# Strassen MLP of a two-layer backbone: in the last chunk pair the second token group goes first, and the block sums of the second matrix no longer trail the chunk pairs

## The chip, the cores and the metric

One core of one Trainium2 chip runs the whole program in one launch. The metric is device time in microseconds (us). The core has a matrix engine (TensorE; PE in the rows, with its weight loads as PEld), two elementwise engines (VectorE, DVE; ScalarE, ACT), GpSimd (POOL), and SyncE (SP), which issues all DMA transfers here, one after the other in its own queue.

## The reference, cut to what matters

Two layers over 1,024 latent and 256 context tokens of width 1,024. Each layer has a token mixer (a gated short convolution in layer 0, a bidirectional mLSTM in layer 1) and then a dense MLP with a squared ReLU; before and after each there is an RMSNorm with shift, scale and gate. Only the MLP matters here:

```
def _sqrelu_mlp(h, w1, w2):
    return jnp.square(jax.nn.relu(h @ w1)) @ w2
```

w1 is 1,024 x 4,096 and w2 is 4,096 x 1,024. Layer 0 runs it on 1,280 tokens, layer 1 on the 1,024 latent ones. Everything is float32.

## The kernel before

Both matrix products of the MLP are done with a Strassen-Winograd scheme: each operand is cut into 2 x 2 blocks, seven products of sums of blocks take the place of eight, and each product is made of three passes over a high part and a rest (so a float32 number goes to TensorE as two pieces).

**The first product** is `mlp_up` (lines 488 to 509). The 4,096 hidden columns are worked off in 16 chunk pairs, q = 0 to 15 (`NQ` = 16); "chunk pair" is a pair of 128-column chunks of w1. The tokens lie in SBUF as two groups of prepared sums, A0 and A1: 384 and 256 columns in layer 0, 256 and 256 in layer 1. In each chunk pair `up_weights` loads two blocks of w1 (`raw`, line 406) and makes seven weight pieces of them (`w`, lines 122 and 123, eight slots); then `up_group` (line 426) runs the seven products for A0 and the seven for A1, each 12 matmuls (line 433), into the PSUM tiles psX, psY, psZ, psW, psX, psZ, psW in that order. ScalarE and VectorE add up, apply the squared ReLU and form seven result pieces in one tile `st` (lines 448 to 468); the transfer on line 469 writes them to `hid_d` in DRAM. A0's group has its `st` in the pool S1, A1's in the pool M, each pool with one buffer: the first write of the next `st` of a pool (line 448, ScalarE) waits until the transfer of line 469 has read the one before.

**Block sums of w2.** `down_sums` (lines 471 to 486) makes the sums that the second product needs: for k = 0 to 15 it loads two rows of w2 (`rw`, line 476, one buffer each), does four VectorE subtractions (lines 480 to 483) and writes the results to `t_d` (lines 484 to 486). The next loads of `rw` wait until these writes have read the buffers. In the loop, chunk pair q does the sums of k = q - 2; those of 14 and 15 come after the loop.

**The second product** is `mlp_down` (from line 511). It takes the seven products one after the other (i = 1, 6, 5, 7, 4, 2, 3); for each it goes through k = 0 to 15: `w_piece` loads a block of w2 or `t_d` (line 521), `h_piece` loads a piece of `hid_d` (`hr`, line 529, three buffers) and makes high part and rest (`hp`, lines 530 and 531, four buffers), and line 536 multiplies them for five pairs of token tiles (layer 0; 15 matmuls for each k) or four (layer 1; 12) into the PSUM tiles `psd`. Lines 544 to 558 empty `psd` at the end of each of the seven.

**What sets the order.** The program is written in the order above, but a scheduler sets the order on each engine; within an engine, and in SP's queue, instructions then run strictly in that order. Memory is given out by a stack of pools: `mlp_up` holds S1 and A1 on the left and A0 and M on the right, and `mlp_down` lays its pools Y and H where S1 and A1 were. H holds `hr` and `hp`, and lies within the place of A1. So the first `hr` loads must wait until the last matmul that reads A1.

Of the kernel before, what the change touches and what calls it, by code (L numbers as in the profile page):

```python
# [37 lines left out]
def hybrid_kernel(  # L38
# [53 lines left out]
    acc = ctx.enter_context(pool("acc", bufs=6, space=PSUM))  # L92
# [306 lines left out]
    NQ = DFF // P // 2  # L399

    def up_weights(l, q, M=None):

        raw = []
        for j in range(2):
            r = rawp.tile([P, 1024], F32, tag="raw", name="raw")
            nc.sync.dma_start(r, w1[l, 2 * q + j])
            raw.append(r)
        (b11, b21), (b12, b22) = [(r[:, 0:512], r[:, 512:1024]) for r in raw]
        if M is None:
            tw = rawp.tile([P, 1024], F32, tag="raw", name="tw0")  # L410
            t2, t3 = tw[:, 0:512], tw[:, 512:1024]
        else:
            t2, t3 = [M.tile([P, 512], F32, tag="tw", name="tw", bufs=2) for _ in range(2)]
        w = {1: piece(b11)}
        nc.vector.tensor_sub(t3, b22, b12)
        nc.vector.tensor_sub(b12, b12, b11)
        nc.vector.tensor_sub(t2, b22, b12)
        w[6] = piece(t2)
        w[5] = piece(b12)
        w[7] = piece(t3)  # L420
        w[2] = piece(b21)
        w[3] = piece(b22)
        nc.vector.tensor_sub(b21, b21, t2)
        w[4] = piece(b21)
        return w

    def up_group(l, q, w, A, n, c0, pl, acc):


        def prod(ps, i, first):  # L430
            for k in range(4):
                for j, (a, b) in enumerate(PASSES):
                    nc.tensor.matmul(  # L433
                        ps,
                        w[i][:, a, k * P : (k + 1) * P],
                        A[:, PIECE[i], b, k, :],
                        start=(first and k == 0 and j == 0),
                        stop=(k == 3 and j == 2),
                        skip_group_check=not first,
                    )  # L440

        bank = lambda nm: acc.tile([P, 512], F32, tag="acc", name=nm)[:, 0:n]
        st = pl.tile([P, 7, n], F32, tag="st7", name="st7", bufs=1)
        r11, r12, r22, c21, u2 = [st[:, i] for i in (0, 1, 2, 5, 6)]
        X, Y, Z, W = bank("psX"), bank("psY"), bank("psZ"), bank("psW")
        add = nc.vector.tensor_add
        prod(X, 1, True)
        nc.scalar.copy(u2, X)  # L448
        prod(Y, 6, True)
        add(u2, Y, u2)  # L450
        prod(Z, 5, True)
        add(r22, Z, u2)  # L452
        prod(W, 7, True)
        add(r22, W, r22)  # L454
        prod(X, 2, False)
        prod(Z, 3, False)
        prod(W, 4, False)
        nc.scalar.activation(r11, X, AF.Relu)
        add(r12, Z, u2)
        add(c21, W, u2)  # L460
        nc.scalar.activation(r11, r11, AF.Square)
        for c in (r22, r12, c21):
            nc.scalar.activation(c, c, AF.Relu)  # L463
            nc.scalar.activation(c, c, AF.Square)
        add(st[:, 3], c21, r22)
        nc.vector.tensor_sub(st[:, 4], st[:, 3], r11)
        nc.vector.tensor_sub(st[:, 5], r11, c21)
        nc.vector.tensor_sub(st[:, 6], r12, st[:, 4])
        nc.sync.dma_start(hid_d[l, :, q, :, c0 : c0 + n].rearrange("s p n -> p s n"), st)

    def down_sums(l, k, M):

        r = []
        for j in range(2):
            r.append(M.tile([P, 1024], F32, tag=f"rw{j}", name="rw", bufs=1))
            nc.sync.dma_start(r[j], w2[l, (2 * k + j) * P : (2 * k + j + 1) * P, :])
        (b11, b12), (b21, b22) = [(x[:, 0:512], x[:, 512:1024]) for x in r]
        t3 = M.tile([P, 512], F32, tag="tw", name="t3", bufs=2)
        sub = nc.vector.tensor_sub
        sub(t3, b22, b12)  # L480
        sub(b12, b12, b11)
        sub(b22, b22, b12)
        sub(b21, b21, b22)
        nc.sync.dma_start(t_d[l, k, :, 3], t3)
        nc.sync.dma_start(t_d[l, k, :, 2], b12)
        nc.sync.dma_start(t_d[l, k, :, 0:2], r[1].rearrange("p (a b) -> p a b", a=2))

    def mlp_up(l, As, sX, left, S1, acc):


        (A0, n0), (A1, n1) = As
        w = up_weights(l, 0)
        up_group(l, 0, w, A0, n0, 0, S1, acc)
        w = up_weights(l, 1)
        for f in left:
            f(A1)
        up_group(l, 1, w, A0, n0, 0, S1, acc)
        sX.close()
        with pool("M", bufs=1, side="right") as M:
            up_group(l, 1, w, A1, n1, n0, M, acc)  # L500
            w = up_weights(l, 0, M)
            up_group(l, 0, w, A1, n1, n0, M, acc)
            for q in range(2, NQ):
                w = up_weights(l, q, M)
                down_sums(l, q - 2, M)
                up_group(l, q, w, A0, n0, 0, S1, acc)
                up_group(l, q, w, A1, n1, n0, M, acc)
            down_sums(l, NQ - 2, M)
            down_sums(l, NQ - 1, M)

    def mlp_down(l, pairs, xsrc, finish, T, H, Y, acc, G):

# [105 lines left out]
    with ExitStack() as s0:  # L618
# [147 lines left out]
        A0 = sA.enter_context(pool("A0", bufs=1, side="right")).tile([P, 7, 2, 4, 384], F32R, name="A0")  # L766
# [12 lines left out]
        with pool("S1", bufs=1) as S1, pool("A1", bufs=1) as pA1:  # L779
            A1 = pA1.tile([P, 7, 2, 4, 256], F32R, name="A1")  # L780
            mlp_up(0, ((A0, 384), (A1, 256)), sX, left, S1, acc)
# [337 lines left out]
    A0 = sA.enter_context(pool("A2", bufs=1, side="right")).tile([P, 7, 2, 4, 256], F32R, name="A2")  # L1119
# [12 lines left out]
    with pool("S3", bufs=1) as S1, pool("A3", bufs=1) as pA1:  # L1132
        A1 = pA1.tile([P, 7, 2, 4, 256], F32R, name="A3")
        mlp_up(1, ((A0, 256), (A1, 256)), sX, left, S1, acc)
# [78 lines left out]
```

## Time and profile before

| | |
|---|---|
| median of 3 runs | 2582.22 us (2580.07 to 2582.91) |
| profiled execution | 2577.89 us |
| its span, first to last instruction | 2576.1 us |
| mean granted TensorE clock | 0.989 of full speed |
| PE busy | 2488.1 us, 97% of the span |
| PEld busy | 2199.3 us, 85% |
| DVE busy | 1651.6 us, 64% |
| ACT busy | 1143.7 us, 44% |
| 16 DMA engines, mean | 177 GB/s |

All times in the views are in us from the start of the span of the one profiled execution. A timeline row gives start, length, engine, line, operation, the tiles written and read, and how many instructions were merged; in square brackets stands how long the engine was idle before it and what ended that. A window row gives, for each engine, busy time and number of instructions, then the granted TensorE clock (1.00 is 2.4 GHz, 0.50 is 1.2 GHz), the busy share of the DMA engines and GB/s. Matmuls overlap: 12 of 128 x 256 start within 1.43 us, though the row that merges them is 1.59 us long.

### The profile page before, as it was taken

How to read it: one execution, taken by the hardware profiler on the slowest of the kernel's cores; microseconds unless marked ns; L12 is line 12 of the kernel's file. 1: busy time of each engine (PE TensorE's matmuls, PEld its weight loads, DVE VectorE, ACT ScalarE, POOL GpSimd, SP SyncE). 2: the span in 40 equal slices, each digit the busy share in tenths (PEclk: the TensorE clock that was granted, in tenths of full speed). 3: DMA queues.
4: the chain of work that ended last, by engine and by line, in shares of the span. 5: the costliest groups of instructions: out<-in, count | busy, mean ns of one | idle time of the engine just before them, and what ended most of it. 6: DMA issues, size and time to landing. Idle time of an engine off the chain costs nothing.

```text
span 2576.1 us, 38825 instructions
## 1 busy us (share of the span) xinstructions
PE 2488.1 (97%) x14520; PEld 2199.3 (85%) x14520; DVE 1651.6 (64%) x3058; ACT 1143.7 (44%) x2503; POOL 107.0 (4%) x229
## 2 busy tenths in 40 slices
PE   8999999999999999999999899999999999999998
PEld 5888887899999988888879788887789999978886
DVE  5777784687676664445864745546578787654565
ACT  5311112565445443334654444345456555444443
POOL 1000000100000000000111100000010000000010
PEclk9999999999999999999999899999999999999999
DMA  8456663436565676555751322222336777876675
GB/s 295 132 175 189 200 194 116 136 127 231 208 242 208 225 268 199 173 167 170 234 185 51 73 78 58 66 74 83 117 126 213 252 246 259 268 239 188 184 230 182
DMA packets 230207, 454.87 MB, mean 177 GB/s; under 512 B 17802, under 2 KB 109242, under 8 KB 230018
## 3 DMA queue, kind: packets, MB, share of 16 engines
q1 hardware_dynamic: 230018, 452.38, 54.2%
q8 instruction: 114, 1.87, 0.3%
q14 instruction: 75, 0.61, 0.1%
HBM read 326.78 MB, written 125.33 MB: 176 GB/s over the span
## 4 chain that ended last, share of the span: by engine, by line
PE 53%; issue 30%; DVE 6%; DMA 6%; ACT 3%; POOL 2%; DVEq 0%; POOLq 0%; SPq 0%; ACTq 0%
PE psd L536 12%; PE op L371 5%; PE psZ L433 4%; PE psW L433 4%; PE psX L433 4%; PE psv L865 3%; PE psc L129 3%; PE pso L129 3%; DMA Dm<-nm_d 3%; PE psb L129 3%; PE psu L129 3%; PE psY L433 2%; DMA mraw<-in_mod_w_dram 2%; PE psq L129 1%; DVE macc L220 1%
## 5 line engine op out<-in xcount | busy, mean ns | idle before, releaser
L536 PE MATMUL psd<-w,hp 128*128 128x512 f32 x3024 | 712.1, 397 | 10.8 <-ACT hp L530 10.8
L536 PEld LDWEIGHTS psd<-w,hp 128*128 128x128 f32 x3024 | 573.5, 190 | 145.7 <-ACT hp L530 11.9
L531 DVE TENSOR_TENSOR hp<-hr,hp 128x512 fp32r<-128x512 f32 (+1 forms) x226 | 169.4, 752 | 255.7 <-ACT hp L530 255.3
L530 ACT CAST hp<-hr 128x512 fp32r<-128x512 f32 (+1 forms) x226 | 151.1, 669 | 330.7 <-PE psd L536 278.0
L123 DVE TENSOR_TENSOR w<-raw,w 128x512 fp32r<-128x512 f32 x394 | 268.2, 685 | 40.9 <-ACT w L122 40.8
L122 ACT CAST w<-raw 128x512 fp32r<-128x512 f32 x394 | 242.5, 617 | 105.6 <-DMA raw<-in_w_dram 37.1
L433 PE MATMUL psX<-A,w 128*128 128x256 f32 (+1 forms) x1536 | 230.0, 298 | 2.2 <-ACT st L448 1.7
L433 PE MATMUL psZ<-A,w 128*128 128x256 f32 (+1 forms) x1536 | 226.8, 296 | 0.2 <-DVE st L452 0.2
L433 PE MATMUL psW<-A,w 128*128 128x256 f32 (+1 forms) x1536 | 226.8, 296 | 0.0
L433 PEld LDWEIGHTS psX<-A,w 128*128 128x128 f32 x1536 | 213.4, 189 | 3.4 <-ACT st L448 2.5
L433 PEld LDWEIGHTS psZ<-A,w 128*128 128x128 f32 x1536 | 211.9, 188 | 0.6 <-DVE st L452 0.5
L433 PEld LDWEIGHTS psW<-A,w 128*128 128x128 f32 x1536 | 211.8, 188 | 0.2 <-DVE st L454 0.2
L371 PE MATMUL op<-w,zs 128*128 128x512 f32 x864 | 206.1, 398 | 5.5 <-ACT zs L365 4.4
L371 PEld LDWEIGHTS op<-w,zs 128*128 128x128 f32 x864 | 162.5, 190 | 42.6 <-ACT zs L365 5.4
L463 ACT ACTIVATE st<-st 128x256 f32<-128x256 f32 (+1 forms) x192 | 85.2, 444 | 226.2 <-DVE st L454 159.0
L220 DVE SCALAR_TENSOR_TENSOR macc<-mraw,sil,macc 128x1024 f32<-128x1024 f32 x112 | 140.6, 1281 | 38.2 <-DMA mraw<-in_mod_w_dram 37.8
L109 ACT CAST w<-raw 128x1024 fp32r<-128x1024 f32 (+1 forms) x73 | 75.5, 1040 | 162.6 <-PE psc L129 61.6
L110 DVE TENSOR_TENSOR w<-raw,w 128x1024 fp32r<-128x1024 f32 (+1 forms) x73 | 87.8, 1209 | 78.7 <-ACT w L109 78.4
L865 PE MATMUL psv<-w,hT 128*128 128x256 f32 (+1 forms) x960 | 134.6, 294 | 0.5 <-ACT V L872 0.5
L865 PEld LDWEIGHTS psv<-w,hT 128*128 128x128 f32 x960 | 124.4, 192 | 1.1 <-ACT V L872 0.9
L433 PE MATMUL psY<-A,w 128*128 128x256 f32 (+1 forms) x768 | 116.0, 297 | 0.0
L129 PE MATMUL psc<-hT,w 128*128 128x512 f32 (+1 forms) x576 | 115.2, 352 | 0.6 <-DVE hT L279 0.4
(242 smaller groups left out, 3445.9 us busy)
## 6 DMA issues: line engine op xcount, KB each, us to landing
hid_d<-st SPq DMA_DIRECT2D x48, 896.0 KB, 5.1
mraw<-in_mod_w_dram SPq DMA_DIRECT2D x80, 512.0 KB, 4.0
raw<-in_w_dram SPq DMA_DIRECT2D x68, 512.0 KB, 3.8
hr<-hid_d SPq DMA_DIRECT2D x104, 320.0 KB, 3.7
rw<-in_w_dram SPq DMA_DIRECT2D x64, 512.0 KB, 5.7
raw<-t_d SPq DMA_DIRECT2D x128, 256.0 KB, 3.1
hr<-hid_d SPq DMA_DIRECT2D x122, 256.0 KB, 2.8
raw<-in_w_dram SPq DMA_DIRECT2D x96, 256.0 KB, 3.8
```

The source lines that it names most:

```text
L110: nc.vector.tensor_sub(w[1], src, w[0].bitcast(F32))
L122: nc.scalar.copy(w[:, 0], src)
L123: nc.vector.tensor_sub(w[:, 1], src, w[:, 0].bitcast(F32))
L129: nc.tensor.matmul(ps, w[a][:, k * P : (k + 1) * P], hold["hT"][:, k, b, t0 : t0 + n], start=(k == 0 and i == 0), stop=(k == KD - 1 and i ...
L220: nc.vector.scalar_tensor_tensor(ac[v], raw, s, ac[v], ALU.mult, ALU.add)
L371: nc.tensor.matmul(ps[h], zs[:, a, k, :], ws[k][b][:, h * 512 : (h + 1) * 512], start=(k == 0 and i == 0), stop=(k == KD - 1 and i == 2),)
L433: nc.tensor.matmul(ps, w[i][:, a, k * P : (k + 1) * P], A[:, PIECE[i], b, k, :], start=(first and k == 0 and j == 0), stop=(k == 3 and j = ...
L463: nc.scalar.activation(c, c, AF.Relu)
L530: nc.scalar.copy(h[:, 0], r)
L531: nc.vector.tensor_sub(h[:, 1], r, h[:, 0].bitcast(F32))
L536: nc.tensor.matmul(ps, h[:, a, o : o + P], w[:, b], start=(first and j == 0), stop=(last and j == 2))
L865: nc.tensor.matmul(ps[:, 0 : self.g], hold["hT"][:, k, a_, t * P : (t + 1) * P], self.wv[k // self.per][b_][:, k % self.per * self.g : (k ...
```

## The change

In the loop of `mlp_up`, the block sums of w2 are counted by `sums_due` instead of q - 2. Chunk pairs 6 and 10 do two of them, so that the count has caught up with q from 10 on and nothing is left to do after the loop. In the last chunk pair (q = 15) the two token groups change places: A1 first, then A0. No arithmetic is added or left out.

```
             up_group(l, 0, w, A1, n1, n0, M, acc)
+            sums_due = 0
             for q in range(2, NQ):
                 w = up_weights(l, q, M)
-                down_sums(l, q - 2, M)
-                up_group(l, q, w, A0, n0, 0, S1, acc)
-                up_group(l, q, w, A1, n1, n0, M, acc)
-            down_sums(l, NQ - 2, M)
-            down_sums(l, NQ - 1, M)
+                for _ in range(2 if q in (6, 10) else 1):
+                    down_sums(l, sums_due, M)
+                    sums_due += 1
+                both = [(A0, n0, 0, S1), (A1, n1, n0, M)]
+                for A, n, c0, pl in both if q < NQ - 1 else both[::-1]:
+                    up_group(l, q, w, A, n, c0, pl, acc)
```

From line 511 on, the line numbers of the changed kernel are two higher (line 536 becomes 538).

What the scheduler makes of this is shown at three places. The first is TensorE at the end of `mlp_up` in layer 0, chunk pair 15 and the first of `mlp_down` (A_3583 is A0, A_4589 is A1; the number behind w is that of the weight piece). Before:

```order
L433 MATMUL psW<-A_3583,w_8648 128x384 x12
L433 MATMUL psX<-A_4589,w_8626 128x256 x12
L433 MATMUL psY<-A_4589,w_8632 128x256 x12
L433 MATMUL psZ<-A_4589,w_8635 128x256 x12
L433 MATMUL psW<-A_4589,w_8638 128x256 x12
L433 MATMUL psX<-A_4589,w_8641 128x256 x12
L433 MATMUL psZ<-A_4589,w_8644 128x256 x12
L433 MATMUL psW<-A_4589,w_8648 128x256 x12
L536 MATMUL psd<-w_8931,hp 128x512 x15
```

and with the change:

```order
L433 MATMUL psW<-A_4589,w_8662 128x256 x12
L433 MATMUL psX<-A_3583,w_8650 128x384 x12
L433 MATMUL psY<-A_3583,w_8656 128x384 x11
L433 MATMUL psX<-A_4589,w_8665 128x256 x12
L433 MATMUL psZ<-A_4589,w_8668 128x256 x12
L433 MATMUL psW<-A_4589,w_8672 128x256 x12
L433 MATMUL psY<-A_3583,w_8656 128x384
L433 MATMUL psZ<-A_3583,w_8659 128x384 x12
L433 MATMUL psW<-A_3583,w_8662 128x384 x12
L433 MATMUL psX<-A_3583,w_8665 128x384 x12
L433 MATMUL psZ<-A_3583,w_8668 128x384 x12
L433 MATMUL psW<-A_3583,w_8672 128x384 x12
L538 MATMUL psd<-w_8931,hp 128x512 x15
```

Before, the last matmul on A1 is the last of `mlp_up`; with the change, one matmul and five products on A0 come between it and `mlp_down`, and two products on A0 are drawn ahead of A1's fifth. In layer 1 it is the same, with two and a third products of A0 drawn ahead and some four and a half left behind.

The second place is SP's queue there (st_8512 and st_8536 are A1's result of chunk pair 14, st_8771 and st_8687 that of 15, raw_8954 to raw_9054 the w2 blocks of `mlp_down`). Before:

```order
L469 DMA hid_d<-st_8512 128x7x256
L476 DMA rw<-in_w_dram 128x1024 x2
L484 DMA t_d<-t_8883 128x512
L485 DMA t_d<-rw 128x512
L486 DMA t_d<-rw 128x1024
L476 DMA rw<-in_w_dram 128x1024
L469 DMA hid_d<-st_8663 128x7x384
L476 DMA rw<-in_w_dram 128x1024
L529 DMA hr<-hid_d 128x640 x3
L469 DMA hid_d<-st_8771 128x7x256
```

and with the change:

```order
L469 DMA hid_d<-st_8536 128x7x256
L523 DMA raw_9029<-in_w_dram 128x512
L531 DMA hr<-hid_d 128x640 x3
L523 DMA raw_9054<-in_w_dram 128x512
L469 DMA hid_d<-st_8687 128x7x256
L531 DMA hr<-hid_d 128x640 x3
```

The transfers for the block sums are gone from the end, and the first `hr` loads stand behind one load of w2 only.

The third place is VectorE in layer 1 where two block sums meet, in chunk pair 6 (st_19163 and st_19175 are A0's results, st_19271 and st_19283 A1's). Before, at the end of A0's group:

```order
L465 TENSOR_TENSOR st_19163<-st_19163 128x256
L466 TENSOR_TENSOR st_19163<-st_19163 128x256
L467 TENSOR_TENSOR st_19163<-st_19163 128x256
L468 TENSOR_TENSOR st_19163<-st_19163 128x256
L123 TENSOR_TENSOR w_19391<-tw,w_19391 128x512
L450 TENSOR_TENSOR st_19271<-psY,st_19271 128x256
L123 TENSOR_TENSOR w_19394<-raw,w_19394 128x512
L452 TENSOR_TENSOR st_19271<-psZ,st_19271 128x256
```

and with the change:

```order
L465 TENSOR_TENSOR st_19175<-st_19175 128x256
L480 TENSOR_TENSOR t_19167<-rw 128x512
L466 TENSOR_TENSOR st_19175<-st_19175 128x256
L481 TENSOR_TENSOR rw<-rw 128x512
L467 TENSOR_TENSOR st_19175<-st_19175 128x256
L482 TENSOR_TENSOR rw<-rw 128x512
L468 TENSOR_TENSOR st_19175<-st_19175 128x256
L483 TENSOR_TENSOR rw<-rw 128x512
L450 TENSOR_TENSOR st_19283<-psY,st_19283 128x256
L415 TENSOR_TENSOR tw<-raw 128x512
L452 TENSOR_TENSOR st_19283<-psZ,st_19283 128x256
```

The second block of sums (lines 480 to 483) stands at the end of A0's group, ahead of lines 450 and 452 of A1's, which free the sums that TensorE's sixth product adds to. The next block, t_19426, then stands just ahead of line 450 of the following A0 group; before, a block always stood in the middle of A1's group.

## Rows read from the trace of the kernel before

**Rows 1.** The page, part 5: the matmuls of the second product.

```profile
L536 PE MATMUL psd<-w,hp 128*128 128x512 f32 x3024 | 712.1, 397 | 10.8 <-ACT hp L530 10.8
```

**Rows 2.** Timeline, layer 0, from mlp_up to mlp_down.

```profile
934.83 1.58 PE L433 MATMUL psW<-A,w 128*128 128x256 f32 x12
...
936.45 1.27 SPq L529 DMA_DIRECT2D hr<-hid_d  x3
...
940.87 19.47 PE L536 MATMUL psd<-w,hp 128*128 128x512 f32 x71 [4.45 <-ACT hp L530]
```

**Rows 3.** Timeline, TensorE in layer 1, from mlp_up to mlp_down.

```profile
2242.80 1.58 PE L433 MATMUL psW<-A,w 128*128 128x256 f32 x12
2248.35 5.49 PE L536 MATMUL psd<-w,hp 128*128 128x512 f32 x12 [3.97 <-ACT hp L530]
2256.19 104.07 PE L536 MATMUL psd<-w,hp 128*128 128x512 f32 x440 [2.35 <-ACT hp L530]
```

**Rows 4.** Lines 544, 546, 548, which empty psd (min/median/max ns, first to last start).

```profile
L544 ACT COPY p<-psd x5: 578/586/600, 997.3 to 999.6; 128x512 f32<-128x512 f32 x5
...
L546 DVE TENSOR_TENSOR u<-psd,p x5: 681/681/691, 1052.6 to 1055.8; 128x512 f32<-128x512 f32 x5
...
L548 DVE TENSOR_TENSOR u<-psd,u x5: 680/681/691, 1108.4 to 1111.5; 128x512 f32<-128x512 f32 x5
...
L544 ACT COPY p<-psd x4: 579/587/592, 2298.1 to 2299.9; 128x512 f32<-128x512 f32 x4
```

**Rows 5.** Timeline, start of mlp_up, layer 0, then layer 1 (two A1 groups).

```profile
550.34 0.67 PE L335 MATMUL pt<-ident,tt 128*128 128x128 f32 x4 [2.11 <-ACT val L338]
...
1961.67 1.22 PE L433 MATMUL psX<-A,w 128*128 128x256 f32 x8 [1.11 <-ACT st L448]
...
1962.77 0.37 ACT L448 COPY st<-psX 128x256 f32<-128x256 f32 x1 [0.22 <-DMA hid_d<-st]
```

**Rows 6.** Windows of 2 us at the two stops of rows 5 (layer 1 first).

```profile
1963.00:1965.00 2.00, 1.92 (x17) 1.80 (x16) 1.93 (x5) 0.22 (x2) 0.00 (x0) 1.00 0.17 68
...
552.00:554.00 2.00, 2.00 (x9) 1.91 (x9) 2.00 (x8) 0.92 (x2) 0.00 (x0) 0.50 0.50 180
```

**Rows 7.** Timeline, chunk pairs 14 to 15; landing times of hid_d, layers 0 and 1.

```profile
911.50 2.27 PE L433 MATMUL psX<-A,w 128*128 128x384 f32 x12
...
915.78 0.38 SPq L469 DMA_DIRECT2D hid_d<-st  x1
...
2224.29 1.58 PE L433 MATMUL psX<-A,w 128*128 128x256 f32 x12
...
2228.27 0.38 SPq L469 DMA_DIRECT2D hid_d<-st  x1
...
hid_d<-st SPq DMA_DIRECT2D x13, 896.0 KB, 5.9
...
hid_d<-st SPq DMA_DIRECT2D x28, 896.0 KB, 4.6
```

**Rows 8.** Timeline and landing time (line 476), one chunk pair of layer 1.

```profile
2126.43 0.33 SPq L486 DMA_DIRECT2D t_d<-rw  x1
...
2131.55 0.33 SPq L476 DMA_DIRECT2D rw<-in_w_dram  x1
...
2136.14 0.43 DVE L465 TENSOR_TENSOR st<-st 128x256 f32<-128x256 f32 x1 [0.93 <-ACT st L464]
...
2141.70 1.59 PE L433 MATMUL psZ<-A,w 128*128 128x256 f32 x12
...
DMA to landing us min/median/max: 5.0/5.3/5.7
```

**Rows 9.** Windows of one chunk pair each, layer 1 and layer 0.

```profile
2124.61:2144.54 19.93, 19.93 (x170) 19.93 (x169) 15.72 (x34) 10.84 (x26) 0.00 (x0) 1.00 0.73 251
...
862.01:886.75 24.74, 24.74 (x170) 24.74 (x169) 16.76 (x34) 11.95 (x26) 0.00 (x0) 1.00 0.64 221
```

**Rows 10.** The page, part 5: a subtraction of the block sums.

```profile
L480 DVE TENSOR_TENSOR t<-rw 128x512 f32<-128x512 f32 x32 | 22.0, 688 | 7.4 <-DMA rw<-in_w_dram 7.0
```

## The prediction

> **What bounds the kernel now.** First the page: TensorE is busy 97% of the span, so time is gained only where it stops or runs slow. The costliest group of matmuls, line 536, has 10.8 us of idle time before it in all, all of it ended by ScalarE writing `hp` [rows 1]. The timeline shows where. In layer 0 the last product of `mlp_up` starts at 934.83 and its row ends at 936.41; SP issues the first `hr` loads at 936.45, right behind it, and the first matmul on `hp` starts at 940.87, after 4.45 idle [rows 2]. That is the memory rule of the kernel at work: `hr` lies on A1, so the loads cannot start before the last matmul on A1, and then the load and two casts pass with TensorE idle. In layer 1 the same stop is 3.97 us, 12 matmuls follow, and it stops again for 2.35 [rows 3]. A stop also costs speed afterwards: those 12 matmuls take 5.49 us.
>
> What this turn from `mlp_up` to `mlp_down` costs in all is read against the steady pace. From one emptying of `psd` to the next, 1052.6 to 1108.4, 240 matmuls take 55.8 us, 0.2325 each [rows 4]. Twelve would take 2.79; 5.49 is about twice that, TensorE at the lower of its two levels (1.2 instead of 2.4 GHz).
>
> **The gain.** In layer 0 the first `psd` is emptied at 997.3, after 228 matmuls [rows 4]. From the end of `mlp_up` (936.41) that is 60.9 us; 228 x 0.2325 is 53.0. So 7.9 go over, less 0.2 for the end of the last matmul: **7.7 us** lost, 4.45 as stop and the rest as slow matmuls. (The 71 matmuls of [rows 2] agree: 19.47 against 16.5.) In layer 1 the first eviction is at 2298.1 [rows 4], 53.7 after 2244.38 [rows 3]; its 183 matmuls are 42.5, so 11.2, less 0.2, **11.0 us**.
>
> With the change A1's last matmul is followed by about 5 products on A0 in layer 0 and 4.6 in layer 1. A product of 256 columns takes 1.424 us (a chunk pair of layer 1 is 14 of them in 19.93 [rows 9]); one of 384 takes 2.11 (24.74 less 7 x 1.424, over 7 [rows 9]). That is some 10.6 us of cover in layer 0 and 6.6 in layer 1, where load and casts took 4.45 and 3.97 [rows 2, 3]. Only one load of w2 stands ahead of `hr` in SP's queue, not five transfers. The second stop of layer 1 comes from the `hr` loads that follow, which started as late as the first; they start earlier too, and the first pieces are there with some 2.6 us of lead. I take both turns as gone: **18.7 us**. Bounds: the 2.35 stop stays (14.3), or all goes.
>
> **A new wait in chunk pair 15.** A1 now follows A1 of chunk pair 14, and both use the one `st` buffer of pool M. Line 448, ScalarE's copy out of psX, waits for the transfer of line 469 to have read the old `st`; behind it TensorE's next product into psX waits. The start of `mlp_up` in layer 1 shows this already: two A1 groups in a row, the copy waits for `hid_d`, and TensorE stops for 1.11 [rows 5]. At the end the scheduler draws products of A0 ahead. Layer 0: A1's group of chunk pair 14 ends at 911.50, its transfer is issued at 915.78 and lands 5.9 later [rows 7]; with the 0.37 copy [rows 5], psX is free at 922.05. TensorE has four products of A1 (5.70) and nearly two of A0 (2.11 and 1.94): 9.75, to 921.25. It stops **0.8**. Layer 1: 2228.27 + 4.6 + 0.37 = 2233.24 [rows 7]; work until 2224.29 + 9.03 = 2233.32. I take **0.2**. Bounds 0 and 1.11 each: with nothing drawn ahead the stop was 1.11, and an early transfer removes it.
>
> **The doubled block sums in layer 1.** In chunk pairs 6 and 10 one block's loads and writes follow another's through single `rw` buffers. Count from the start of A0's group (2124.61). The second load stood behind the writes by 5.12 us (2126.43 to 2131.55), so it goes out at +6.9 and lands 5.3 later, +12.2 [rows 8]. Its four subtractions, 0.69 each [rows 10], stand with lines 466 to 468 (0.43 each [rows 8]) between line 465 (+11.5) and line 450 of A1's group. So line 450 starts at about +16.3, and line 452, behind it and line 415, ends at about +17.8. TensorE wants that sum for the product at 2141.70, +17.1 [rows 8]: up to 0.7 late. Next, the second block's writes start at +16.4 and let go of `rw` at +21.5; the third load lands at +26.8. Its subtraction stands ahead of line 450 of the next A0 group, so line 452 there ends at about +29.0, where TensorE wants it at 19.93 + 5 x 1.424 = +27.05. That is 1.9 late; since the first delay moves this need back too, the two together are some **1.7 us** a place, **3.4** for both. Bounds: 0 (the queue of SP or the landing a little ahead) and 4 a place. VectorE as a whole has room: busy 15.72 of 19.93 [rows 9], and four more subtractions make 18.5, 93%.
>
> I take TensorE's clock as unhurt by these: after the 1.11 stop it stayed at 1.00, while after the 2.11 stop in layer 0 it stood at 0.50 [rows 5, 6]. The stops here are each nearer the first, but 1.9 isn't far from the second; the price if it falls is in the upper bound.
>
> **In layer 0** the same chain has 24.74 us a chunk pair, 4.8 more, and VectorE is busy 16.76 of it [rows 9]. The 1.9 of lateness is covered: **0**, with bounds of 0 and 1.1 a place. What leaves the end of `mlp_up`, two blocks of transfers and subtractions, stood on no path to the end (VectorE and ScalarE waited for `hr` there): 0, apart from the earlier `hr`.
>
> **Sum.** 18.7 - 1.0 - 3.4 = **14.3 us** less. The profiled execution took 2577.89, so 2563.6; it lies 4.3 under the median of the runs, 2582.22, to which I carry the gain: **2567.9**.
>
> **Rivals.** *Transfers land later in the doubled chunk pairs.* Two blocks' transfers in one chunk pair meet the weights' and results' traffic; the share of the DMA engines is 0.73 already [rows 9]. The same kind of transfer, 896 KB, landed in 4.6 in layer 1 and 5.9 in layer 0 [rows 7], so 1.3 to 1.5 more is seen. Write and load in series make that 3 us at each place of layer 1, and 0.5 of it shows at each of layer 0: 14.3 - 7 = 7.3, **2575**. Against it: the load landed in 5.0 to 5.7 in all its rows [rows 8]. Chance 0.12. The Trainium skill, "DMA: Bandwidth & Descriptors", section "Latency and other measured facts", gives HBM's access latency as 0.2 us on average and 2 at high load; by that rule, as an estimate, each of the two transfers could land 1.8 later, 3.6 a place, and the time would be some 2576. The narrow 5.0 to 5.7 at a share of 0.73 speaks against that here.
>
> *Slower: VectorE, which works in order, is held by a subtraction that waits for `rw`, twice at each of the four places, long enough for the clock to halve.* The 2.35 stop of layer 1 shows the price: of 11.0 lost there, 3.97 and 2.7 (5.49 - 2.79) belong to the first stop, which leaves 4.3 for the second. Two such at each place of layer 1 are 17.2, one at each of layer 0 8.6; with 2.2 at the ends the cost is 28.0 against 18.7: slower by 9.3, **2591.5**. It decides from the point at which the loads and writes of `rw` take about 2 us longer than 5.3 and 5.1. Nothing in the rows does; chance 0.05.
>
> *The change doesn't do what it says*: the first `hr` loads are still late, held in SP's queue behind the load of w2 that waits for its buffer, so that most of the turns' cost stays and the rest pays the new waits: about **2582**. Against it: only one transfer stands ahead, and the layer has 6.6 us of cover for 4 to 4.5 of work. Chance 0.07.
>
> **How the numbers follow.** The forecast has 0.76. Some 0.2% (5.2 us) is what a measurement of this kernel tells from no change. Forecast and most of the first rival are faster by more (0.86); the third and the rest of the first lie within (0.08); the second, and a little of the third, are slower (0.06). The range begins where the new waits cost nothing (2563.5) less 2 for the spread of the runs, 2561.5, and ends at the first rival and the bounds of 4 a place with a slow clock once, 2576.5.
>
> **What would show it.** Right: in both layers `psd`'s first matmul follows the last product of `mlp_up` with no idle time and the clock at 1.00; `hr` is issued 6 to 11 us before it; line 448 waits for `hid_d` in chunk pair 15 with TensorE idle under 1.1; in layer 1, near chunk pairs 6 and 10, TensorE stops 1 to 2 us at psZ for line 452, and not in layer 0; no block sums after the loop. Wrong: line 538 still idles for `hp`; a stop over 2 us with the clock at 0.50 at the doubled places; VectorE idle for `rw` at line 480 for several us; or stops in products that the change did not touch.

## The result and the profile after

The changed kernel took 2562.85 us (median of 4 runs, 2559.49 to 2567.07) beside 2581.14 for the kernel before (4 runs, 2579.71 to 2582.91). The ratio is 0.993, with a 95% interval of 0.9911 to 0.9948: 18 us less, between 13 and 23. Forecast were 14.3 less and 2567.9. Two later measurements of the same kernel gave 0.9943 and 0.9941 (14.7 and 15.2 less). Here and below, a gain in us is the ratio's distance from 1 times the median of the kernel before.

The profiled execution took 2567.07, the longest of its four, and that of before 2577.89, under its shortest; so their spans (2565.3 and 2576.1) differ by 10.8 only. Where such a difference lies can be told by marks that both traces have. From the last eviction of the first layer to the first product of `mlp_up` in the second, where the change touches nothing, before took 563.0 us, this execution 566.6, and the executions of all the kernels below between 558.4 and 569.2: a scatter of 10.8, as much as the larger of the two turns gave. So the terms are read stage by stage.

First the page's group of matmuls of the second product, then the timeline of the two turns from `mlp_up` to `mlp_down`, as in [rows 1 to 3]:

```profile
L538 PE MATMUL psd<-w,hp 128*128 128x512 f32 x3024 | 706.7, 395 | 0.6 <-DVE p L558 0.6
```

```profile
923.25 1.68 SPq L531 DMA_DIRECT2D hr<-hid_d  x3
...
931.69 2.27 PE L433 MATMUL psW<-A,w 128*128 128x384 f32 x12
...
933.80 6.46 PE L538 MATMUL psd<-w,hp 128*128 128x512 f32 x27
...
2237.38 1.27 SPq L531 DMA_DIRECT2D hr<-hid_d  x3
...
2242.28 1.58 PE L433 MATMUL psW<-A,w 128*128 128x256 f32 x12
...
2243.71 18.52 PE L538 MATMUL psd<-w,hp 128*128 128x512 f32 x79
```

The 10.8 us of waiting for `hp` are gone, 0.6 for something else is left. `hr` is issued 10.6 and 6.3 us before the first matmul on it, and that matmul follows `mlp_up` with no stop, in both layers. Behind layer 1's turn the granted clock was at its lower level before and is at full speed now; two windows of 2 us, before and after:

```profile
2250.00:2252.00 2.00, 2.00 (x7) 1.52 (x6) 1.59 (x3) 0.00 (x0) 0.00 (x0) 0.50 0.94 328
...
2244.00:2246.00 2.00, 2.00 (x10) 1.64 (x9) 1.63 (x5) 1.62 (x5) 0.00 (x0) 1.00 1.00 333
```

The first evictions (the copies that empty `psd`), which [rows 4] had at 997.3 and 2298.1:

```profile
L546 ACT COPY p<-psd x5: 577/588/599, 987.6 to 990.0; 128x512 f32<-128x512 f32 x5
...
L546 ACT COPY p<-psd x4: 581/587/587, 2286.8 to 2288.5; 128x512 f32<-128x512 f32 x4
```

From the end of `mlp_up` that is 987.6 - 933.96 = 53.6 us where before took 60.9, and 2286.8 - 2243.86 = 42.9 where it took 53.7. The turns gave **7.3 and 10.8 us**.

What the change cost shows in two places. At the end of `mlp_up` in layer 0 (TensorE, SP and ScalarE, timeline):

```profile
912.49 0.38 SPq L469 DMA_DIRECT2D hid_d<-st  x1
...
918.26 0.37 ACT L448 COPY st<-psX 128x256 f32<-128x256 f32 x1 [1.04 <-DMA hid_d<-st]
...
918.69 1.69 PE L433 MATMUL psX<-A,w 128*128 128x256 f32 x12 [0.56 <-ACT st L448]
```

The copy waits for the transfer of A1's previous `st`, and TensorE stops for 0.56. In layer 1 it doesn't stop there. The other place is chunk pair 6 of layer 1:

```profile
2042.16 1.59 PE L433 MATMUL psY<-A,w 128*128 128x256 f32 x12
...
2045.13 3.25 SPq L476 DMA_DIRECT2D rw<-in_w_dram  x2
...
2052.12 1.59 PE L433 MATMUL psY<-A,w 128*128 128x256 f32 x12
...
2054.25 0.69 DVE L480 TENSOR_TENSOR t<-rw 128x512 f32<-128x512 f32 x1 [1.56 <-DMA rw<-in_w_dram]
...
2057.67 0.42 DVE L450 TENSOR_TENSOR st<-psY,st 128x256 f32<-128x256 f32 x1
...
2058.60 0.42 DVE L452 TENSOR_TENSOR st<-psZ,st 128x256 f32<-128x256 f32 x1
2059.07 1.69 PE L433 MATMUL psZ<-A,w 128*128 128x256 f32 x12 [1.09 <-DVE st L452]
...
2063.45 1.58 PE L433 MATMUL psY<-A,w 128*128 128x256 f32 x12
...
2067.67 0.69 DVE L480 TENSOR_TENSOR t<-rw 128x512 f32<-128x512 f32 x1 [0.28 <-DMA rw<-in_w_dram]
...
2069.68 1.68 PE L433 MATMUL psZ<-A,w 128*128 128x256 f32 x12 [0.39 <-DVE st L452]
...
2074.05 1.59 PE L433 MATMUL psY<-A,w 128*128 128x256 f32 x12
```

VectorE stands 1.56 us at the second block's first subtraction, for `rw`; lines 450 and 452 come behind it, and TensorE waits for line 452, twice. The groups, read from one psY to the next, take 11.33 and 10.60 us instead of 9.97: 2.0 us. At chunk pair 10 the same reading gives 0.65, of which 0.2 is a slower pace told of in the last section. No stop shows at the doubled places of layer 0.

### The profile page after: what moved, and what is told of

The parts are those of the page before. It is cut to its first block, busy times and chain, and to the rows that moved or that the text cites. A ratio compares the mean times of both kernels' runs of the same rounds, so it can differ in the third digit from the quotient of the medians.

```text
span 2565.3 us, 38800 instructions
## 1 busy us (share of the span) xinstructions
PE 2485.2 (97%) x14520; PEld 2194.7 (86%) x14520; DVE 1649.5 (64%) x3058; ACT 1141.6 (45%) x2503; POOL 107.0 (4%) x229
## 4 chain that ended last, share of the span: by engine, by line
PE 51%; issue 30%; DVE 7%; DMA 7%; ACT 3%; POOL 2%; DVEq 0%; SPq 0%; POOLq 0%; ACTq 0%
PE psd L538 11%; PE op L371 5%; PE psZ L433 4%; PE psW L433 4%; PE psX L433 4%; PE psv L867 3%; PE pso L129 3%; DMA Dm<-nm_d 3%; PE psc L129 3%; PE psb L129 2%; PE psu L129 2%; DMA mraw<-in_mod_w_dram 2%; PE psY L433 2%; PE psq L129 1%; DVE macc L220 1%
```

## The experiments

All are edits of the changed kernel, timed beside the kernel before on the same chip.

**The changed kernel again (1), and once more (10).**

> The changed kernel as it is, timed beside the others. Theory (the turns from the first to the second product are worth 18.7 us, the back-to-back A1 groups cost 0.6, the doubled block sums about 1.5 in chunk pair 6 of layer 1 alone): 15 to 18 us less than before, ratio 0.993 to 0.994. Rival (the doubled places cost 3.4 as forecast, and some executions go better by chance): 13 to 15 less, 0.9945. TensorE stops for 1.1 and 0.4 us near chunk pair 6 of layer 1 again, if that stop belongs to the program, and not near chunk pair 10.

> The changed kernel a third time, beside the two kernels with second buffers. Theory: 14.5 to 17 us less than before; near chunk pairs 6 and 10 of layer 1 stops at psZ of 1 to 1.5 and 0 to 0.6 us. Rival (the earlier two stops there were chance): none.

Measured: 0.9943 (0.9928 to 0.9958) and 0.9941 (0.9928 to 0.9955). Experiment 1's timeline (TensorE, VectorE and SP) at chunk pair 10 of layer 1:

```profile
2122.40 3.30 SPq L476 DMA_DIRECT2D rw<-in_w_dram  x2
...
2129.41 1.59 PE L433 MATMUL psY<-A,w 128*128 128x256 f32 x12
...
2130.20 0.69 DVE L480 TENSOR_TENSOR t<-rw 128x512 f32<-128x512 f32 x1 [0.23 <-DMA rw<-in_w_dram]
...
2133.62 0.42 DVE L450 TENSOR_TENSOR st<-psY,st 128x256 f32<-128x256 f32 x1
...
2145.65 1.69 PE L433 MATMUL psZ<-A,w 128*128 128x256 f32 x12 [0.28 <-DVE st L452]
...
2150.02 1.58 PE L433 MATMUL psY<-A,w 128*128 128x256 f32 x12
```

At chunk pair 6 its stops were 0.66 and 0.42 (1.6 us by the groups); at 10, 0.28 (2150.02 - 2129.41, less two groups of 9.97: 0.7). Experiment 10 had 0.64, 0.26 and none: 1.4 and 0.3. (It also had one of 0.93 in chunk pair 4, at 2003.51, behind a VectorE that had waited 0.96 for the load of the weights; experiment 2 had one of 0.62 there.) So the stop at 6 belongs to the program; at 10 VectorE waited 0.23 for `rw`, where it had waited 1.13 at 6 in the same execution, and the place costs less than half. Both halves of experiment 1's theory missed: 14.7 lies under its 15 to 18, and there was a stop at 10.

**Only the change of places (2); only the catch-up (3).**

```
-                for _ in range(2 if q in (6, 10) else 1):
-                    down_sums(l, sums_due, M)
-                    sums_due += 1
+                down_sums(l, q - 2, M)
...
+            down_sums(l, NQ - 2, M)
+            down_sums(l, NQ - 1, M)
```

> Only the last chunk pair changes places; the block sums keep trailing, two after the loop. Theory (the gain comes from A1's earlier last matmul alone): the first psd matmul follows mlp_up with hardly a stop in layer 0, where the first load of hr stands behind one write of the block sums only; some idle time may come back at the second and third piece, whose loads stand behind two and three more: 12 to 17 us less than before. Rival (the block sums at the end must go as well, or hr stays late in SP's queue behind writes that wait for VectorE): stops of 2 us or more with the clock at 0.50 at hp in both layers, 5 to 10 us less.

```
-                for A, n, c0, pl in both if q < NQ - 1 else both[::-1]:
+                for A, n, c0, pl in both:
```

> Only the block sums catch up; in the last chunk pair A0 still goes first. Theory: hr still waits for A1's last matmul, so the stops of 4 to 4.5 us at both turns stay; 0 to 3 us less for fewer transfers there, 1.5 to 3.4 more for the doubled places: between 3 less and 3 more. Rival (the trailing block sums made the turns slow): 8 to 12 less.

Measured: 0.996 (0.9947 to 0.9974), 10.3 us less, for the first, just above the rival's range; 0.9982 (0.9972 to 0.9993), 4.6 less, for the second, more than the 3 that its theory allowed. The timeline of experiment 2 in layer 1:

```profile
2228.53 1.69 PE L433 MATMUL psX<-A,w 128*128 128x256 f32 x12 [0.87 <-ACT st L448]
...
2233.25 0.32 SPq L531 DMA_DIRECT2D hr<-hid_d  x1
2233.67 0.37 SPq L486 DMA_DIRECT2D t_d<-rw  x1
2234.13 0.39 SPq L476 DMA_DIRECT2D rw<-in_w_dram  x1
...
2238.16 2.10 SPq L531 DMA_DIRECT2D hr<-hid_d  x2
...
2239.58 2.95 PE L538 MATMUL psd<-w,hp 128*128 128x512 f32 x12
...
2244.76 17.45 PE L538 MATMUL psd<-w,hp 128*128 128x512 f32 x66 [2.23 <-ACT hp L532]
```

In layer 0 the theory held: no stop at `hp`, the first eviction 53.7 after `mlp_up` (986.6 - 932.9). In layer 1 the rival did: the first `hr` goes out early, the second and third 4.9 us later, behind four transfers of results and block sums in SP's queue (two of them are shown), and TensorE stops after one piece. Its turn there lost 8.1 us (2290.5 - 2239.74, less the 42.7 of a turn without loss). Experiment 3 keeps the first stop:

```profile
937.45 1.33 PE L538 MATMUL psd<-w,hp 128*128 128x512 f32 x3 [3.71 <-ACT hp L532]
```

```profile
2254.29 75.98 PE L538 MATMUL psd<-w,hp 128*128 128x512 f32 x317 [4.62 <-ACT hp L532]
```

but the second stop of [rows 3], 2.35, is gone: 7.1 us are lost in layer 1's turn instead of 11.0. So there each half alone gives some 3 to 4 us, and only both together give 10.8. In layer 0's turn the first eviction came 59.6 after `mlp_up` instead of 60.9, so the catch-up alone gave 1.3 there.

**Two blocks left out (4).** The price of the doubled places, measured by taking them away; the output is not the reference's, since the second product reads sums 13 for 14 and 15.

```
-                for _ in range(2 if q in (6, 10) else 1):
...
+                down_sums(l, q - 2, M)
...
-            nc.sync.dma_start(r, src[i] if i in src else t_d[l, k, :, {4: 0, 6: 1, 5: 2, 7: 3}[i]])
+            nc.sync.dma_start(r, src[i] if i in src else t_d[l, min(k, NQ - 3), :, {4: 0, 6: 1, 5: 2, 7: 3}[i]])
```

> The last chunk pair changes places; block sums k = 14 and 15 are left out (the second product reads those of 13 in their place, transfers of the same size), so there is neither a doubled place nor a sum after the loop. Theory: 18 us less than before (18.7 less 0.6 of the A1 stop in layer 0), no stop near chunk pair 6, and 1.5 to 2 less than the changed kernel. Rival (the doubled places cost more than their stops show, through a slower pace after them): 3 or more less than the changed kernel.

Measured: 0.9923 (0.991 to 0.9937), 19.9 less, 5 less than experiment 1, though the intervals of the two meet. The traces give less: no stop at psZ in layer 1, and from its first product to the second pass of evictions 418.4 us against 421.1 in experiment 1, so 2.7. Layer 0 has no difference behind its start: from the second group of chunk pair 4 to that pass, 390.8 in both.

**A second rw buffer in layer 1 (5, and again 11).**

```
-            r.append(M.tile([P, 1024], F32, tag=f"rw{j}", name="rw", bufs=1))
+            r.append(M.tile([P, 1024], F32, tag=f"rw{j}", name="rw", bufs=1 + l))
```

> The changed kernel with two buffers for each rw tile in layer 1 (its pool M has room there). Theory (the price of a doubled place is the chain through the single rw buffers: write 5.1 us, load 5.3, subtractions in VectorE's order): no stop at psZ near chunk pairs 6 and 10 of layer 1, 2 to 3 us less than the changed kernel, 17 to 19 less than before. Rival (VectorE or the DMA engines have no room for two blocks in one chunk pair, whatever the buffers): the stops stay, the same as the changed kernel within 1 us.

> The changed kernel with two rw buffers of each kind in layer 1, again, beside the changed kernel on the same chip. Theory: 2 to 3 us less than the changed kernel and no stop at psZ. Rival (the 4 us between the two measurements so far were mostly chance): within 1 us of the changed kernel.

Measured: 0.9924 (0.991 to 0.9938) and 0.9929 (0.9917 to 0.9941), 19.6 and 18.3 less. VectorE at chunk pair 6 of layer 1 in experiment 5:

```profile
2032.60 0.69 DVE L480 TENSOR_TENSOR t<-rw 128x512 f32<-128x512 f32 x1
2032.71 0.33 SPq L486 DMA_DIRECT2D t_d<-rw  x1
```

The second block's first subtraction runs 0.11 us before the first block's last write is even issued; it waits for nothing, and TensorE has no stop at psZ in `mlp_up` of layer 1, in either execution. The groups keep 9.97 at both doubled places. So the stops come from the single `rw` buffers: VectorE and the DMA engines do have room for two blocks in one chunk pair. (With the second buffer the scheduler also placed the block earlier on VectorE, so its wait and its place went together.) Beside the changed kernel on the same chip the median is 2.6 lower (2558.93 against 2561.56), as expected, though the intervals overlap.

**The doubled pairs side by side (6).**

```
-                for _ in range(2 if q in (6, 10) else 1):
+                for _ in range(2 if q in (6, 7) else 1):
```

> The two doubled chunk pairs stand side by side, 6 and 7 instead of 6 and 10. Theory (chain): four blocks want some 4 x 14.6 us (load 5.3, subtractions some 4, write 5.1) through single buffers in two chunk pairs of 19.9 or 24.7: TensorE stops at psZ in several groups of layer 1 after chunk pair 6, 5 to 12 us in all, and now in layer 0 too, up to 4; 4 to 12 us more than the changed kernel. Rival (only a doubled place's own instructions on VectorE count): no more stops than with 6 and 10, the same as the changed kernel within 1 us.

Measured: 0.9966 (0.9953 to 0.9979), 8.8 less than before, so some 6 more than the changed kernel. TensorE in layer 1, behind the two stops of chunk pair 6 (0.76 and 0.26):

```profile
2087.27 1.10 PE L433 MATMUL psX<-A,w 128*128 128x256 f32 x7 [0.73 <-ACT st L448]
...
2094.97 1.71 PE L433 MATMUL psZ<-A,w 128*128 128x256 f32 x12 [0.66 <-DVE st L452]
...
2136.49 2.53 PE L433 MATMUL psZ<-A,w 128*128 128x256 f32 x12 [1.82 <-DVE st L452]
```

The lateness is carried over several chunk pairs, since each block's write and load must end before the next; and layer 0 has a stop now (0.21 at psZ). After the stop of 1.82 the granted clock was 0.50 from 2138 to 2140, and the 12 matmuls took 2.53 instead of 1.59. With the same number of instructions on VectorE, the distance between the doubled places decides.

**No doubled place: sums 0 and 1 at the start (7).**

```
             w = up_weights(l, 0, M)
+            down_sums(l, 0, M)
             up_group(l, 0, w, A1, n1, n0, M, acc)
+            down_sums(l, 1, M)
...
+                down_sums(l, q, M)
```

> No doubled place: the block sums of k = 0 and 1 go into the two A1 groups at the start of the first product, chunk pair q then does those of k = q, and the last chunk pair changes places as in the changed kernel. Theory (the price of the doubled places is all that is left to gain): 2 to 3 us less than the changed kernel, 17 to 20 less than before, the stops at the start (1.0 us at psX in layer 1) no longer. Rival (at the start two blocks' transfers meet the weights' and the first results'): longer stops at the start of layer 1 or 0, 3 us or more, so no better or worse than the changed kernel.

Measured: 1.0012 (1.0002 to 1.0022), 0.1% slower than before, and some 18 us behind the changed kernel. The rival held, and more than expected. In layer 1:

```profile
1967.11 0.32 SPq L486 DMA_DIRECT2D t_d<-rw  x1
1967.48 0.44 SPq L406 DMA_DIRECT2D raw<-in_w_dram  x1
...
1973.72 0.62 ACT L122 CAST w<-raw 128x512 fp32r<-128x512 f32 x1 [0.89 <-DMA raw<-in_w_dram]
...
1976.61 0.69 DVE L480 TENSOR_TENSOR t<-rw 128x512 f32<-128x512 f32 x1
1977.21 0.68 DVE L415 TENSOR_TENSOR tw<-raw 128x512 f32<-128x512 f32 x1
...
1982.21 0.80 PE L433 MATMUL psY<-A,w 128*128 128x256 f32 x2 [9.33 <-ACT w L122]
```

The load of chunk pair 2's weights stands behind the block sums' writes in SP's queue, and the four subtractions of the next block stand among VectorE's steps that make the weight pieces. TensorE waits 9.33 us for a piece (7.76 in layer 0, at 603.81), and restarts at the lower clock: the window from 1984 to 1986 has 0.50.

**The places changed from chunk pair 14 on (8).**

```
-                for A, n, c0, pl in both if q < NQ - 1 else both[::-1]:
+                for A, n, c0, pl in both if q < NQ - 2 else both[::-1]:
```

> The two token groups change places in chunk pairs 14 and 15, not in 15 alone. Theory (the stop of 0.3 to 0.9 us in chunk pair 15 of layer 0 comes from two A1 groups in a row through the one st buffer): it moves to chunk pair 14, where A1 follows A1 of 13; none stays in 15, where A1 now follows A0; the turns stay as in the changed kernel; the same time within 1.5 us. Rival (the stop in 15 comes from work that crowds the end of mlp_up): it stays in 15.

Measured: 0.9936 (0.9922 to 0.995), 16.5 less. The stops moved with the two A1 groups:

```profile
895.98 1.69 PE L433 MATMUL psX<-A,w 128*128 128x256 f32 x12 [0.47 <-ACT st L448]
```

```profile
2210.25 1.70 PE L433 MATMUL psX<-A,w 128*128 128x256 f32 x12 [1.26 <-ACT st L448]
```

and none is left in 15. In layer 1 it is 1.26 now, where the changed kernel had none.

**Second buffers for rw and st in layer 1 (9).**

```
-        st = pl.tile([P, 7, n], F32, tag="st7", name="st7", bufs=1)
+        st = pl.tile([P, 7, n], F32, tag="st7", name="st7", bufs=1 + (l if c0 else 0))
```

> The changed kernel with two rw buffers of each kind and two st buffers in pool M, both in layer 1 alone. Theory (each of the two waits goes with its second buffer): no stop at psZ after the doubled places, none at psX at the start of layer 1 (1.0 us in the changed kernel), the 0.3 to 0.6 in chunk pair 15 of layer 0 stays: 18.5 to 21 us less than before, 3 to 4 less than the changed kernel. Rival (at the start of layer 1 the weights are late anyway): the stop there only changes its releaser; 2 to 3 less than the changed kernel.

Measured: 0.9935 (0.9915 to 0.9954), 16.8 less; its median, 2558.59, is that of experiment 11 (2558.93). The stop at the start of layer 1 is gone, but a new one of 0.33 at psZ (1979.30) stands shortly behind; from the first product to the first eviction layer 1 takes 372.8 us against 373.7 and 373.8 in the executions with the `rw` buffers alone. One microsecond in the trace, nothing in the measured time, and short of the 18.5 to 21 expected, within a wide interval. The version with second `rw` buffers is the better one to keep: two measurements put it at 18 to 20 less than before.

## Why the prediction was right

**The turns, 18.7 forecast, 18.1 measured** (7.3 and 10.8 against 7.7 and 11.0). The working by the steady pace was right, and it mattered: the idle time alone, the 10.8 of [rows 1], would have given little more than half. The 0.6 missing is that the first pass still ran 0.4 and 0.2 over 228 and 183 matmuls at the even pace. The mechanism, `hr` waiting for A1's last matmul, is shown by experiment 3, which keeps A0 first and keeps the first stops.

**What the end of mlp_up loses, 0 forecast.** As a term of the sum it did no harm. But its reason (those transfers "stood on no path to the end") holds for the first `hr` only, and the reading that the later `hr` loads of layer 1 "started as late as the first" is wrong. SP's queue in layer 1 before:

```profile
2244.41 0.32 SPq L529 DMA_DIRECT2D hr<-hid_d  x1
...
2251.06 0.32 SPq L484 DMA_DIRECT2D t_d<-t  x1
...
2252.16 0.43 SPq L529 DMA_DIRECT2D hr<-hid_d  x1
```

The second `hr` went out 7.75 us after the first, behind transfers of the block sums; that, and not A1, made the second stop of [rows 3]. Experiment 3 takes the trailing block sums away and this stop goes, with A1 still last; experiment 2 leaves them, and 2.23 us of stop stay, 8.1 lost in the turn. So the catch-up is no tidying beside the real change; without it some 8 of layer 1's 10.8 are missing. The prediction saw that fewer transfers stand ahead of `hr`, but tied the second stop to A1; that its 11.0 for layer 1 came true is owed to the catch-up, which was part of the change.

**Two A1 groups in a row, 1.0 forecast, 0.6 measured** (0.56 and none; 0.24 to 0.66 in layer 0 over the executions). Experiment 8 moved the stop with the groups, so two A1 groups in a row are the cause, and the copy that TensorE waits for itself waits for the transfer out of `st`.

**Doubled places in layer 1, 3.4 forecast, 2.3 measured in experiment 1** (1.6 and 0.7; 2.0 and 0.4 in the first execution, the slower pace taken off; 1.4 and 0.3 in experiment 10). The chain through `rw` is right: experiment 5 removes the stops with a second buffer, experiment 6 crowds the blocks and makes them longer. But two of its terms were mis-sized, and at chunk pair 6 they nearly cancelled. There, counted from the start of A0's group at 2040.73, line 450 started at +16.9 (forecast +16.3) and the third block's subtraction at +26.9 (+26.8). The second block's load, though, went out at +7.3 (the later of the two transfers at 2045.13), and from there to the end of VectorE's wait it took 6.1 us, not 5.3 (6.9 and 6.0 in experiments 1 and 10). And from line 480 to line 450 VectorE took 3.4 us (2054.25 to 2057.67), not the 4.1 that the prediction got by adding the lengths of rows, which overlap here. At chunk pair 10 of experiment 1 the load went out 0.4 later than counted and landed in 4.7, so that line 480 started at +12.2, as forecast; line 450 came 0.7 earlier than forecast, at +15.6, and TensorE had no stop in that group. The third block's subtraction came at +25.6 instead of +26.8: 0.7 of this are the shorter steps, the rest its write and load, which took 9.9 us and not 10.4. So where the load arrived as counted, a place cost 0.3 to 0.7 us and not 1.7, and that chunk pair 6 came near the forecast is in part luck. Why its load was late was not found.

**Layer 0's doubled places, 0 forecast:** no stop in any execution of the changed kernel.

**The sum:** 18.1 - 0.6 - 2.3 = 15.2 us, against 14.3 forecast and 18.1, 14.7 and 15.2 measured. (The 18.1 of the turns and the 0.6 are from the first execution, the 2.3 from experiment 1.) All three terms came out a little smaller than forecast, the gain by 0.6 and the costs by 1.5. The 18.1 of the first measurement, beside the 14.7 and 15.2 of the later two, is scatter that no term explains.

Of the rivals, late transfers came in part. Of the four loads at the doubled places, the second block's at chunk pair 6 landed 0.7 to 1.6 us later than counted, as said; the other three landed in 3.9 to 4.9 us, earlier than the 5.3. The Trainium skill, "DMA: Bandwidth & Descriptors", section "Latency and other measured facts", gives HBM's access latency as 0.2 us on average and 2 at high load; the prediction's estimate from it was 1.8 more for each transfer. The trace does not agree for three of the four loads, though the DMA engines were busy 0.93 to 0.98 of the time, in windows of 5 us, while the third blocks were loaded. No stop at a doubled place of the changed kernel passed 1.09 us, and the clock at both turns stood at 1.00, so neither the clock rival nor the late `hr` came.

## What to carry to other kernels

A stop of TensorE at a change of stage is priced by the work done from its start to a mark well behind it against the steady pace, not by its idle time, since the matmuls after the stops at the turns ran at half speed here. A wait that comes from memory that is used again can be lifted by changing who reads that memory last, but the transfers that stand ahead in the queue must leave too: half the change gave little in layer 1. When single-buffered work is doubled up, count write, load and arithmetic per block as a chain, take the arithmetic from start to start and not by adding lengths, and look first whether a second buffer fits.

## What was not expected

The stop for `val` at the start of `mlp_up` in layer 0 ([rows 5], 2.11 us) was 1.84 to 2.04 in the executions after, and its length did not decide what TensorE's clock did after it. In experiment 2, after 1.96, all windows of 2 us show 1.00; in experiment 10, after 1.96 too, they show 0.77, 0.50 and 0.88. It is worth 1.3 us: from that stop to the second group of chunk pair 4, 103.8 us in experiment 2 and 105.1 in the changed kernel's first profile.

In some executions the same matmuls ran 1.1% slower for a long stretch, a product every 1.44 us instead of 1.424, with the granted clock shown as 1.00 in all windows of both. TensorE in the changed kernel's first profile, ahead of the point and behind it:

```profile
2132.44 1.58 PE L433 MATMUL psX<-A,w 128*128 128x256 f32 x12
2133.86 1.59 PE L433 MATMUL psY<-A,w 128*128 128x256 f32 x12
...
2146.91 1.60 PE L433 MATMUL psW<-A,w 128*128 128x256 f32 x12
2148.35 1.60 PE L433 MATMUL psX<-A,w 128*128 128x256 f32 x12
```

It began at 2139.6 and lasted to about 2234, ten us before the end of `mlp_up`; experiment 1, the same kernel, had it only from 2135 to 2145. Experiments 2, 6 and 7 had it for 100 us and more, each after a stop of TensorE; but other stops were not followed by it. What sets it was not found; with 0.11 us a group it adds up to 3 us to an execution.
